# Local attention: mask added by VectorE, probabilities scaled ahead of transposing, values stationary in column halves, and a new order of the mixer

## The chip, the cores and the metric

The kernel runs on one core of a Trainium2 chip. The metric is the device time of one execution in microseconds. Three executions of the kernel before gave 978.89, 980.45 and 980.59 us; the median is 980.45 us. A trace was taken of one further execution.

## What is computed

The reference is a two-layer encoder on 256 positions of width 1024. Each layer is a half-step feed-forward block, a mixer, and a second half-step feed-forward block, each followed by a layer norm:

```python
x = layer_norm(ALPHA * x + 0.5 * swiglu(x, ffn1_w_in[l], ffn1_w_out[l]), ln_g[l, 0], ln_b[l, 0])
mix = hybrid_mixer(x, cos, sin, mask, w_in[l], w_out[l], ...)
x = layer_norm(ALPHA * x + mix, ln_g[l, 1], ln_b[l, 1])
x = layer_norm(ALPHA * x + 0.5 * swiglu(x, ffn2_w_in[l], ffn2_w_out[l]), ln_g[l, 2], ln_b[l, 2])
```

The mixer projects x to two groups of heads and applies rotary positions. The first group is differential attention (4 heads, each with two score maps). The second is local attention: 8 query heads in two groups of 4, one key and value head for each group, a window of 128 positions to either side, and a sink logit for each query head that takes part in the softmax's maximum and sum. The two results stand side by side and go through one output projection:

```python
s = jnp.where(mask[None, :, None, None, :, :], s, -jnp.inf)
m = jnp.maximum(jnp.max(s, axis=-1, keepdims=True), sk)
e = jnp.exp(s - m)
p = e / (jnp.sum(e, axis=-1, keepdims=True) + jnp.exp(sk - m))
o = jnp.einsum('bnhgqk,bnkhd->bnqhgd', p.astype(v.dtype), vb)
```

## The kernel before

The 256 positions are two tiles t of 128 rows. Activations that a matmul takes as its stationary operand lie transposed in `xx`, which holds for each of the 8 chunks k of the width a rounded high part and the remaining low part. Every weight tile of 128x1024 is loaded by a DMA from SyncE's queue (L72), rounded by ScalarE to `wh` (L74), and its rest is taken by VectorE as `wl` (L75); these two run at a lowered priority. A product is then three matmuls: high by high, high by low, low by high. `raw` has 5 buffers, `wh` and `wl` have 9 each, and a weight is asked for 8 tiles ahead.

TensorE's order is the program's own order. The other engines' order is set by the scheduler of the framework, with a few blocks raised in priority.

The mixer's order on TensorE is the table `ORDER` (L47 to L54). Its words are: `P nm t c`, c quarter-projections (L448 to L450) of dq, dk, dv, sq or sk for tile t; `T`, the transposing of a projected and rotated tile (`transp`, L475); `S d` and `S s`, scores of the differential (`sd`) and of the local group (`ss`), 4 heads' maps in a unit u; `A`, transposing of the differential probabilities; `V`, their product with the values (`od`); `W q n`, three steps of the local group's product with the values for tile q; `Y t h`, transposing of half h of the mixer's result y into `xx`; `O t c`, c of the 8 chunks of the output projection (`ao`, L666); `X` and `Z`, transposing of x; `G`, loading of the norm's factors.

The lines the change touches:

- `swa_scores` (L516): a unit is 12 matmuls for 4 maps in two PSUM banks, one bank for each key head v. Key head 0 lies on partitions 0 to 63, key head 1 on 64 to 127, so that the matmuls of the two (L486) use different row halves of the array. After the 3 matmuls of a map, a matmul of `identb` with the bf16 `mask` (L525), on all 128 rows, adds minus 2^100 to the masked block. VectorE takes the maxima (L528), ScalarE the exponentials and their sums (L542), VectorE the reciprocal of the sums (L545, L546).
- `swa_pv` (L582): unscaled exponentials are transposed (L554), copied to `pTs` by ScalarE (L556), and used as the stationary operand; the values `vs` stream past with 64 columns (L598, 16 matmuls in float32 for a tile). VectorE multiplies the result by the reciprocals and writes it to y (L613). `Y t 1` then transposes that half of y (L260), and ScalarE and VectorE write its two parts to `xx` (L262, L263).
- the start: `load_xt` (L156) brings x transposed in four pieces of two chunks, each followed by one weight tile; the positions and the rotary frequencies are loaded by GpSimd's queue (L191, L193).
- the rotary arithmetic of a projection is `rope` (L454 to L473), at the ordinary priority.

## Time and profile before

| | |
|---|---|
| median of three runs | 980.45 us (978.89 to 980.59) |
| the profiled execution | 979.31 us, span of its trace 977.5 us |
| TensorE matmul busy | 966.5 us, 99% |
| TensorE weight load busy | 823.5 us, 84% |
| VectorE busy | 664.6 us, 68% |
| ScalarE busy | 510.6 us, 52% |
| GpSimd busy | 18.3 us, 2% |
| bytes moved by DMA | 176.44 MB, 181 GB/s on average |

A matmul's row in the trace lasts longer than the next one has to wait, since matmuls are pipelined. What a matmul costs is therefore read from the distance between the start of one and the start of the next, not from its length; the same holds, to a lesser degree, for VectorE and ScalarE, where rows overlap by some 0.08 us.

### The profile page before, as it was taken

Reading aid. Unit: us, or ns where it says so; the run is one execution under the profiler, and the core shown is the slowest. Engines: PE = TensorE matmul, PEld = TensorE weight load, DVE = VectorE, ACT = ScalarE, POOL = GpSimd, SP = SyncE. Lnnn points to the kernel's source line nnn. Section 1 sums busy time; section 2 is a strip of 40 time slices with the busy share of each in tenths; the row PEclk is TensorE's granted clock in tenths of the full one; section 3 lists DMA queues with packets and bytes.
Section 4 is the critical chain, followed back from the end, with each engine's and each line's share of the span. In section 5 each row is a group of like instructions: output and inputs, shape, how many; then the busy total and the mean of one; then the engine's idle time right before and its main releaser. Section 6 shows DMA issues by size and latency. Waiting matters only on the chain.

```text
span 977.5 us, 13872 instructions
## 1 busy us (share of the span) xinstructions
PE 966.5 (99%) x5199; PEld 823.5 (84%) x5199; DVE 664.6 (68%) x1057; ACT 510.6 (52%) x887; POOL 18.3 (2%) x30
## 2 busy tenths in 40 slices
PE   8999999999999999999999999999999999999997
PEld 5888888888888888888888888888888888888886
DVE  6887654598838766664587667548896587766534
ACT  4767553346744655553356555433576456555420
POOL 1000000000000000000000000000000000000000
PEclk9999999999999999999999999999999999999999
DMA  7986555375305755555377555554742167555521
GB/s 267 317 291 195 193 176 192 128 237 194 109 25 162 269 191 185 186 190 194 113 243 248 187 184 191 187 193 128 250 137 76 44 230 248 190 193 186 181 65 44
DMA packets 50323, 176.44 MB, mean 181 GB/s; under 512 B 5824, under 2 KB 7376, under 8 KB 50256
## 3 DMA queue, kind: packets, MB, share of 16 engines
q1 hardware_dynamic: 50192, 175.54, 53.4%
q8 instruction: 41, 0.67, 0.3%
q0 software_dynamic: 64, 0.02, 0.1%
q14 instruction: 26, 0.21, 0.1%
HBM read 174.48 MB, written 1.05 MB: 180 GB/s over the span
## 4 chain that ended last, share of the span: by engine, by line
PE 98%; DMA 1%; DVE 1%; SPq 0%; ACT 0%; issue 0%; DVEq 0%
PE acc L383 24%; PE hg L333 14%; PE hu L333 14%; PE hb L301 9%; PE hu L335 7%; PE hg L335 7%; PE ao L666 5%; PE ss L486 2%; PE os L598 1%; DMA raw<-in_f_b_dram 1%; PE pj_sq L448 1%; PE pj_sq L450 1%; PE pj_dq L450 1%; PE pj_dq L448 1%; PE pj_sq L449 1%; PE pj_dv L448 1%
## 5 line engine op out<-in xcount | busy, mean ns | idle before, releaser
L75 DVE TENSOR_TENSOR wl<-raw,wh 128x1024 fp32r<-128x1024 f32 (+1 forms) x317 | 385.3, 1219 | 209.4 <-ACT wh L74 205.3
L74 ACT CAST wh<-raw 128x1024 fp32r<-128x1024 f32 (+1 forms) x317 | 331.8, 1049 | 324.7 <-PE acc L383 123.7
L383 PE MATMUL acc<-wh,g 128*128 128x512 f32 (+1 forms) x748 | 192.7, 377 | 0.0
L383 PEld LDWEIGHTS acc<-wh,g 128*128 128x128 f32 x748 | 136.0, 188 | 25.8
L333 PE MATMUL hg<-xx,wh 128*128 128x512 f32 x576 | 144.8, 393 | 0.0
L333 PE MATMUL hu<-xx,wh 128*128 128x512 f32 x576 | 144.2, 392 | 0.0
L333 PEld LDWEIGHTS hg<-xx,wh 128*128 128x128 f32 x576 | 103.6, 189 | 18.6
L333 PEld LDWEIGHTS hu<-xx,wh 128*128 128x128 f32 x576 | 103.6, 189 | 18.5
L383 PE MATMUL acc<-wl,g 128*128 128x512 f32 (+1 forms) x374 | 111.3, 377 | 0.0
L335 PEld LDWEIGHTS hg<-xx,wl 128*128 128x128 f32 x576 | 78.6, 190 | 5.7
L335 PEld LDWEIGHTS hu<-xx,wl 128*128 128x128 f32 x576 | 78.6, 190 | 5.6
L335 PE MATMUL hu<-xx,wl 128*128 128x256 f32 x576 | 80.3, 282 | 0.0
L335 PE MATMUL hg<-xx,wl 128*128 128x256 f32 x576 | 80.3, 282 | 0.0
L383 PEld LDWEIGHTS acc<-wl,g 128*128 128x128 f32 x374 | 68.9, 188 | 13.2
L301 PE MATMUL hb<-wh,xx 128*128 128x512 f32 x256 | 72.7, 401 | 2.2 <-ACT wh L74 2.2
L301 PEld LDWEIGHTS hb<-wh,xx 128*128 128x128 f32 x256 | 49.0, 193 | 14.3 <-ACT wh L74 4.3
L301 PE MATMUL hb<-wl,xx 128*128 128x512 f32 x128 | 40.4, 398 | 0.3 <-DVE wl L75 0.3
L666 PE MATMUL ao<-wh,xx 128*128 128x512 f32 x128 | 37.7, 398 | 0.0
L342 ACT CAST g<-tl 128x256 fp32r<-128x256 f32 x72 | 28.9, 402 | 6.8 <-DVE tl L340 6.8
L340 DVE TENSOR_TENSOR tl<-tl 128x256 f32<-128x256 f32 x72 | 30.6, 425 | 2.3
L337 DVE TENSOR_TENSOR tl<-hu,tl 128x256 f32<-128x256 f32 x72 | 30.1, 417 | 2.2 <-ACT tl L336 2.2
L343 DVE TENSOR_TENSOR g<-tl,g 128x256 fp32r<-128x256 f32 x72 | 30.1, 419 | 2.0 <-ACT g L342 1.9
(184 smaller groups left out, 980.8 us busy)
## 6 DMA issues: line engine op xcount, KB each, us to landing
raw<-in_f_in_dram SPq DMA_DIRECT2D x144, 512.0 KB, 3.8
raw<-in_f_out_dram SPq DMA_DIRECT2D x88, 512.0 KB, 3.5
raw<-in_m_in_dram SPq DMA_DIRECT2D x36, 512.0 KB, 3.6
raw<-in_f_b_dram SPq DMA_DIRECT2D x31, 512.0 KB, 3.5
raw<-in_m_out_dram SPq DMA_DIRECT2D x16, 512.0 KB, 4.4
lng<-in_ln_g_dram SPq DMA_DIRECT2D x6, 512.0 KB, 5.7
lnb<-in_ln_b_dram SPq DMA_DIRECT2D x6, 512.0 KB, 5.8
xr<-in_x_tr_dram SPq DMA_DIRECT2D x4, 256.0 KB, 8.7
```

What stands on the lines that cost most here:

```text
L74: nc.scalar.copy(wh[:, s], raw[:, s])
L75: nc.vector.tensor_tensor(wl[:, s], raw[:, s], wh[:, s].bitcast(F32), ALU.subtract)
L301: mm(hb[s], xx[:, k, g, t, :], ww[:, 512 * s : 512 * s + 512], start=(k == 0 and e == 0), stop=(k == KT - 1 and e == 2))
L333: mm(hs[s], wh[:, k * P : (k + 1) * P], xx[:, k], start=(k == 0), stop=False)
L335: mm(hs[s][:, 1, :], wl[:, k * P : (k + 1) * P], xx[:, k, 0], start=False, stop=(k == KT - 1))
L337: dv.tensor_tensor(tl[:, s], hs[s][:, 0, :], tl[:, s], ALU.add)
L340: dv.tensor_tensor(gv, tl[:, 0], gv, ALU.mult)
L342: nc.scalar.copy(gs[q][:, jj, 0, :], gv)
L343: dv.tensor_tensor(gs[q][:, jj, 1, :], gv, gs[q][:, jj, 0, :].bitcast(F32), ALU.subtract)
L383: mm(a, g, ww[:, s], start=(k == 0 and e == 0), stop=(k == JT - 1 and e == 2))
L448: mm(o, xx[:, k, 0, t, :], wh[:, s], start=(k == 0), stop=False)
L666: mm(acc[t][h], xx[:, k, g, t, :], ww[:, s], start=(k == 0 and e == 0), stop=(k == KT - 1 and e == 2))
```

## The change

The core of the diff:

```diff
-identb = cp.tile([P, P], BF16, name="identb")
-nc.gpsimd.tensor_copy(identb, ident)
-mask = cp.tile([P, 2, P], BF16, name="mask")
+mask = cp.tile([P, 2, P], F32, name="mask")
...
-                        qk(sc[v][:, i, :], sqT, skT, a, 2 * u + i, 0, qt, False)
-                        mm(sc[v][:, i, ob], identb, mask[:, qt, :], start=False, stop=True)
+                        qk(sc[v][:, i, :], sqT, skT, a, 2 * u + i, 0, qt)
                 mx = sp.tile([P, 4], F32, tag="mx", name=f"mxs{nm}")
                 for v in range(2):
+                    mb = mask[:, qt : qt + 1, :].to_broadcast([P, 2, P])
+                    dv.tensor_tensor(sc[v][:, :, ob], sc[v][:, :, ob], mb, ALU.add)
                     dv.tensor_reduce(mx[:, 2 * v : 2 * v + 2], sc[v], AX.X, ALU.max)
...
                 dv.reciprocal(rc, rc)
-            return e, rc
+                for v in range(2):
+                    for i in range(2):
+                        q = 2 * v + i
+                        dv.tensor_scalar(e[:, v, i, :], e[:, v, i, :], rc[:, q : q + 1], None, ALU.mult)
+            return e
...
-                        mm(o[:, hd, :], pTs[q][:, i, k, :], vs[:, k, v * HD : (v + 1) * HD], start=(k == 0), stop=(k == 1))
+            def mm_(u):
+                for k in range(2):
+                    for v in range(2):
+                        a = slice(v * HD, (v + 1) * HD)
+                        mm(o[a, 2 * u : 2 * u + 2, :], vs[:, k, a], pTs[u, v][:, :, k, :], start=(k == 0), stop=(k == 1))
...
-                        for u, (e, rc) in enumerate(units):
-                            rv = rc.rearrange("p (v i) -> p v i", v=2)[:, :, :, None].to_broadcast([P, 2, 2, HD])
-                            dv.tensor_tensor(yv[:, :, u], ov[:, :, u], rv, ALU.mult)
+                        dh = xx[:, 4:8, 0, qt, :]
+                        nc.scalar.copy(dh, o)
+                        dv.tensor_tensor(xx[:, 4:8, 1, qt, :], o, dh.bitcast(F32), ALU.subtract)
...
+        def rope(*a):
+            with tc.high_priority():
+                return rope_(*a)
...
-    for c in range(4):
-        load_xt(c)
-        W.upto(c + 1)
+    for k0, k1 in ((0, 1), (1, 2), (2, 4), (4, 6), (6, 8)):
+        load_xt(k0, k1)
+        W.upto(k1)
...
     def rotary():
+        nc.sync.dma_start(pos_i, pos)
+        nc.sync.dma_start(inv_t, inv.partition_broadcast(P))
```

In words: the 32 mask matmuls go, and VectorE adds the mask in PSUM, two additions for a unit. VectorE multiplies the exponentials by the reciprocals ahead of their transposing, four multiplications for a unit. In the product with the values, the values are now the stationary operand, 64 columns of them for each key head, so that the two key heads' results come on partitions 0 to 63 and 64 to 127 of one bank, already transposed; the probabilities stream past with 256 columns, 8 matmuls for a tile. ScalarE and VectorE write that straight to `xx`, and `Y t 1` with its transposes is gone. The rows of the output projection's weight that belong to this half are gathered to match, by two DMAs of 64 partitions for a tile. The first two chunks of x come in pieces of their own, the positions and frequencies are loaded later, from SyncE's queue, and the rotary arithmetic is raised in priority. `ORDER` is another table; its last part is now

```python
A 0 1; T sq 0; T sk 0; V 0; S s 0; P sq 1 1; A 1 1; A 1 0; P sq 1 1; S s 0; V 1; Y 0; G; T sq 1; O 0
2; S s 1; W 0 0; O 0 1; Y 1; W 0 1; W 0 2; O 0 1; S s 1; O 1 1; W 1 0; O 0 1; O 1 1; O 0 1; W 1 1; O 0 2; W 1 2;
O 1 4; Z; O 1 2
```

On TensorE, the first local score unit of layer 0 stands so in the program before (`ss0000` and `ss0001` are the banks of the two key heads, `identb` the identity that the mask goes through):

```order
L486 MATMUL ss0000_2510<-skT0_1865,sqT00_1863 128x256 x2
L486 MATMUL ss0000_2510<-skT0_1865,sqT01_1864 128x256
L525 LDWEIGHTS identb_142
L525 MATMUL ss0000_2510<-mask_144,identb_142 128x128
L486 MATMUL ss0001_2511<-skT0_1865,sqT00_1863 128x256 x2
L486 MATMUL ss0001_2511<-skT0_1865,sqT01_1864 128x256
L525 LDWEIGHTS identb_142
L525 MATMUL ss0001_2511<-mask_144,identb_142 128x128
```

and so in the changed program, ahead of a quarter of sq's projection for the second tile:

```order
L497 MATMUL ss0000_2496<-skT0_1867,sqT00_1865 128x256 x2
L497 MATMUL ss0000_2496<-skT0_1867,sqT01_1866 128x256
L497 MATMUL ss0001_2497<-skT0_1867,sqT00_1865 128x256 x2
L497 MATMUL ss0001_2497<-skT0_1867,sqT01_1866 128x256
L455 MATMUL pj_0_sq1_2438<-wh82_1997,xx_78 128x512
```

The matmuls of the two row halves now follow each other with nothing between (the first rows of the block, which come twice in a unit, are shown once).

On VectorE, between the rotation of sq for the second tile (`m1`, `m2`, `r_0_sq1`) and the low part of its transposed form (`sqT01`), the program before has these rows around the second score unit (`mxs001` are its maxima, `wl92` a split of a weight, `y01` the differential group's result for the second tile):

```order
L75 TENSOR_TENSOR wl92_2573<-raw92_2571,wh92_2572 128x1024
L470 TENSOR_TENSOR r_0_sq1_2560<-m1_0_sq1_2558,m2_0_sq1_2559 128x2x4x64
L528 TENSOR_REDUCE mxs001_2628<-ss0010_2610 128x2
L575 TENSOR_SCALAR f01_2585<-sq01_2584 128x4
L528 TENSOR_REDUCE mxs001_2628<-ss0011_2611 128x2
```

and the changed program has these:

```order
L80 TENSOR_TENSOR wl91_2420<-raw91_2418,wh91_2419 128x1024
L470 TENSOR_TENSOR m1_0_sq1_2559<-pj_0_sq1_2438,cos_t_182 128x512
L473 TENSOR_TENSOR m2_0_sq1_2560<-pj_0_sq1_2438,sin_t_183 128x8x32 x2
L539 TENSOR_TENSOR ss0010_2566<-ss0010_2566,mask_170 128x2x128
L477 TENSOR_TENSOR r_0_sq1_2561<-m1_0_sq1_2559,m2_0_sq1_2560 128x2x4x64
L540 TENSOR_REDUCE mxs001_2580<-ss0010_2566 128x2
L539 TENSOR_TENSOR ss0011_2567<-ss0011_2567,mask_170 128x2x128
L557 TENSOR_TENSOR rs000_2526<-ds000_2521,es000_2516 128x4
L80 TENSOR_TENSOR wl92_2652<-raw92_2650,wh92_2651 128x1024
L270 TENSOR_TENSOR xx_78<-tr_y000_2630,xx_78 128x4x128
```

A mask addition has come between the rotation's parts, and the split of weight 92 stands ahead of the low part of the first transposed y (`xx_78<-tr_y000`), which the output projection takes.

Further on in VectorE's list of the changed program, the scaling of the first two units' probabilities (`esw000`, `esw001`) has these places:

```order
L558 RECIPROCAL rs000_2526<-rs000_2526 128x4
L492 TENSOR_TENSOR sqT01_1866<-tq_0_sq1_2641,sqT00_1865 128x4x128
L562 TENSOR_SCALAR esw000_2520<-esw000_2520,rs000_2526 128x256 x4
L557 TENSOR_TENSOR rs001_2596<-ds001_2591,es001_2586 128x4
L539 TENSOR_TENSOR ss0100_2674<-ss0100_2674,mask_170 128x2x128
L539 TENSOR_TENSOR ss0101_2675<-ss0101_2675,mask_170 128x2x128
```

The four multiplications of a unit are new in the list, and the transposes of `W 0 0` and `W 0 1` read what they write.

More of the change, by code (lines that the diff above doesn't have):

```diff
@@ L69, in _make @@
         n = 512 if i == 0 else 1024
+        src = self.srcs[i]
+        rows = src if isinstance(src, tuple) else (src,)
         for c in range(0, 1024, n):
             s = slice(c, c + n)
-            nc.sync.dma_start(raw[:, s], self.srcs[i][:, s])
+            for q, r in enumerate(rows):
+                h = P // len(rows)
+                nc.sync.dma_start(raw[q * h : (q + 1) * h, s], r[:, s])
             with self.tc.high_priority(-LATER):
@@ L134, in encoder_kernel @@
         srcs += [m_in[l, 3, q] for q in range(4)]
-        srcs += [m_out[l, k * P : (k + 1) * P, :] for k in range(KT)]
+        srcs += [m_out[l, k * P : (k + 1) * P, :] for k in range(KT // 2)]
+        srcs += [tuple(m_out[l, 512 + 256 * v + HD * n : 512 + 256 * v + HD * (n + 1), :] for v in range(2))
+                 for n in range(KT // 2)]
         srcs += [f2_b[l, k] for k in range(KT)]
@@ L481, in transp, with qk @@
             dv.tensor_tensor(dst[1][:, :, a], tr[:, 0:n, :], dst[0][:, :, a].bitcast(F32), ALU.subtract)
-        def qk(o, q, k, a, h, kh, qt, last):
+        def qk(o, q, k, a, h, kh, qt):
             b = slice(qt * P, (qt + 1) * P)
             for i, (m, n) in enumerate(((0, 0), (0, 1), (1, 0))):
-                mm(o, q[m][a, h, b], k[n][a, kh, :], start=(i == 0), stop=(last and i == 2))
+                mm(o, q[m][a, h, b], k[n][a, kh, :], start=(i == 0), stop=(i == 2))
         def diff_scores(qt, u):
@@ L654, in do_w @@
             if n == 0:
-                sw[q] = swa_pv(q, units["s", q], y[q])
+                sw[q] = swa_pv(q, units["s", q])
             sw[q](n)
@@ L692, in mixer @@
             elif op == "W":
-                ok = num("S", "s", ar[0]) > min(ar[1], 1) and (ar[1] == 0 or num("W", ar[0], ar[1] - 1))
+                ok = (ar[1] < 2 or all(full(nm, ar[0]) for nm in heads)) and num("S", "s", ar[0]) > min(ar[1], 1) and (ar[1] == 0 or num("W", ar[0], ar[1] - 1))
             elif op == "Y":
-                ok = all(full(nm, ar[0]) for nm in heads) and (num("W", ar[0], 2) if ar[1] else num("V", ar[0]))
+                ok = all(full(nm, ar[0]) for nm in heads) and num("V", ar[0])
             elif op == "O":
-                ok = num("Y", ar[0], 0) and num("G") and (rows(ar[0]) + ar[1] <= 4 or num("Y", ar[0], 1))
+                ok = num("Y", ar[0]) and num("G") and (rows(ar[0]) + ar[1] <= 4 or num("W", ar[0], 2))
             elif op == "Z":
```

50 lines of the change are left out of this document (18 added, 32 removed).

## The prediction

> **What bounds the kernel now.** I read the page first (span, busy shares, the chain that ended last), then TensorE's waits after the start, then TensorE's timeline in the mixer, and at last the rows of VectorE, which gets the new work.
>
> ```profile
> span 977.5 us, 13872 instructions
> PE 966.5 (99%) x5199; PEld 823.5 (84%) x5199; DVE 664.6 (68%) x1057; ACT 510.6 (52%) x887; POOL 18.3 (2%) x30
> PE 98%; DMA 1%; DVE 1%; SPq 0%; ACT 0%; issue 0%; DVEq 0%
> ```
>
> The waits of TensorE between 15 and 977 us have one row:
>
> ```profile
> PE hb L301 <- DVE wl L75: 0.3, 1, 0.3
> ```
>
> So TensorE sets the time: 98% of the chain is its matmuls, and after the first 15 us it waits 0.3 us in all. A matmul taken from its list is worth the distance from its start to the next start, as long as no other engine comes to be late. Every saving must be set against what VectorE then does.
>
> **The change part by part.** These are starts and lengths of TensorE's rows in layer 0:
>
> ```profile
> 230.72 0.39 PE L449 MATMUL pj_dv<-wl,xx 128*128 128x512 f32 x1
> 230.94 0.39 PE L450 MATMUL pj_dv<-wh,xx 128*128 128x512 f32 x1
> ...
> 231.26 0.98 PE L486 MATMUL sd<-dkT,dqT 64*128 64x256 f32 x12
> ...
> 232.17 0.39 PE L448 MATMUL pj_sk<-wh,xx 128*128 128x256 f32 x1
> 232.39 0.28 PE L449 MATMUL pj_sk<-wl,xx 128*128 128x256 f32 x1
> 232.51 0.28 PE L450 MATMUL pj_sk<-wh,xx 128*128 128x256 f32 x1
> ...
> 250.95 1.97 PE L568 MATMUL od<-vd,pTd 128*128 128x128 f32 x16
> 252.67 0.47 PE L448 MATMUL pj_sq<-wh,xx 128*128 128x512 f32 x1
> ...
> 255.10 0.62 PE L486 MATMUL ss<-skT,sqT 64*128 64x256 f32 x3
> 255.65 0.23 PE L525 MATMUL ss<-mask,identb 128*128 128x128 bf16 x1
> ...
> 257.84 0.61 PE L260 MATMUL tr_y<-ident,y 128*128 128x128 f32 x4
> 258.20 0.47 PE L448 MATMUL pj_sq<-wh,xx 128*128 128x512 f32 x1
> ...
> 273.46 3.68 PE L598 MATMUL os<-vs,pTs 128*128 128x64 f32 x32
> 276.98 0.61 PE L260 MATMUL tr_y<-ident,y 128*128 128x128 f32 x4
> ```
>
> *The masks.* A differential unit and a local unit have the same 12 matmuls on alternating row halves; only the masks stand between the local ones. The first takes 232.17 - 231.26 = 0.91 us, or 0.08 a matmul; the second takes 257.84 - 255.10 = 2.74 us. Its first three matmuls take 0.55, or 0.18 each, so the masks cost more than their own 0.16: they keep the two halves from overlapping. Without them a local unit should cost what the differential one does. Leaving the half-array also costs something: the matmul behind `sd` waits 232.39 - 232.17 = 0.22, where 0.12 is usual (232.51 - 232.39); a masked unit ended on the full array and did not pay it. The saving is 2.74 - 0.91 - 0.10 = 1.73 us for each of 8 units: **-13.8**.
>
> The Trainium skill, page "TensorEngine Tiling (Array Packing)", section Key Properties, says that switching the tiling mode drains TensorE, which speaks for removing the masks and against the new column halves. The trace bears it out: the 0.10 above, and 231.26 - 230.94 = 0.32 at the entry against 230.94 - 230.72 = 0.22. Without the rule, 8 x 0.10 here and the 1.2 of the column halves below would fall away, and the sum would be 2.0 lower.
>
> *Transposes of y's second half.* Four blocks of 258.20 - 257.84 = 0.36 us go, one for each tile and layer: **-1.4**. ScalarE's and VectorE's writing to `xx` is the same in kind and number.
>
> *Values stationary in halves.* The old product of a tile has 32 rows (two for each float32 matmul) and takes 276.98 - 273.46 = 3.52 us. The new one has 8 matmuls, so 16 rows, with 256 columns in float32, a form the trace does not have:
>
> ```profile
> L568 PE MATMUL od<-vd,pTd 128*128 128x128 f32 x64 | 7.8, 275 | 0.0
> L449 PE MATMUL pj_sk<-wl,xx 128*128 128x256 f32 x32 | 9.1, 283 | 0.0
> ```
>
> A float32 row of 128 columns lasts about as long as a rounded one of 256, so I take a float32 row of 256 columns to cost what a rounded one of 512 does, 0.22 (the low end is 0.12, that of 256). Without overlap that is 16 x 0.22 = 3.5, no gain. But pairs of rows lie on the two column halves in turn, as triples in `sd` lie on the row halves. If a row starts, in order, as soon as its own half is free, 12 rows in triples fill 9 steps of 0.91 / 9 = 0.10, which fits the 0.12 of a lone row better than 6 steps of 0.15 would; and 8 rows in pairs fill 5 steps. Two groups of 8 then cost 10 x 0.22 = 2.2. The new blocks switch mode at both ends; there are 3 a layer (one tile's two steps stand together), so 6 x 2 x 0.10 = 1.2 in all. With overlap: 4 x (3.52 - 2.2) - 1.2 = 4.1, **-4.1**; without it 1.2 slower; with the low price and overlap 4 x (3.52 - 1.2) - 1.2 = 8.1 faster. I take the overlap at 0.22, by the `sd` row.
>
> *VectorE.* It gets 16 mask additions and 32 multiplications and loses 8 products (L613). Where that matters is the stretch of the mixer's end. Its rows there, and the busy time of TensorE, its weight loads and VectorE in 10 us windows:
>
> ```profile
> 232.65 1.28 DVE L499 TENSOR_REDUCE mxd<-sd 128x2 f32<-128x512 f32 x2
> 248.75 0.75 DVE L466 TENSOR_TENSOR m_sq<-pj_sq,sin_t 128x256 f32<-128x256 f32 x2
> 254.49 0.17 DVE L575 TENSOR_SCALAR f<-sq 128x4 f32<-128x4 f32 x1
> 254.57 0.15 DVE L622 TENSOR_TENSOR nlam<-le 128x1 f32<-128x1 f32 x1
> 255.99 1.13 DVE L580 SCALAR_TENSOR_TENSOR y<-od,f,gsb 128x128 f32<-128x128 f32 x4
> 301.24 3.49 DVE L75 TENSOR_TENSOR wl<-raw,wh 128x1024 fp32r<-128x1024 f32 x3
> ...
> 250.00:260.00 10.00, 10.00 (x68) 8.39 (x67) 8.79 (x22) 6.65 (x19) 1.02 (x1) 1.00 0.38 118
> 260.00:270.00 10.00, 10.00 (x63) 8.11 (x62) 7.25 (x24) 6.92 (x25) 1.01 (x1) 1.00 0.26 98
> 270.00:280.00 10.00, 10.00 (x75) 8.50 (x75) 4.29 (x14) 4.81 (x18) 0.00 (x0) 1.00 0.02 4
> ```
>
> VectorE is 88% and 73% busy in the windows where the first local scores fall, and 43% in the next. I take the stretch from the first local scores to the transposes of `W 0 1`, and count VectorE's list of the changed program there: 6 mask additions at 0.75 / 2 = 0.38 (2.3); 6 maxima at 0.64 (3.8); 8 products for y at 0.28 (2.2); 2 weight splits at 1.16 (2.3); the rotation of sq, two at 0.64 and two at 0.38 (2.0); 2 low parts at 0.64 (1.3); 8 multiplications; 20 small ones at 254.57 - 254.49 = 0.08 (1.6). A multiplication by a column has its bounds here:
>
> ```profile
> L427 DVE TENSOR_SCALAR gsb<-gsb 128x128 f32<-128x128 f32 x2 | 0.4, 222 | 2.1 <-DMA gsb<-in_sub_g_dram 2.1
> L513 DVE SCALAR_TENSOR_TENSOR ed<-ed,wt 128x256 f32<-128x256 f32 x16 | 7.0, 480 | 0.1
> DVE f L578 <- POOL f L576: 3.0, 4, 1.1
> ```
>
> 0.22 with half the columns, 0.48 with the same columns and two inputs; I take 0.30, nearer the first since it is the same operation (8 x 0.30 = 2.4). GpSimd's power makes VectorE wait 3.0 / 4 = 0.75 a time, twice; as other rows stand between, I take half (0.7). The sum is 18.6 us.
>
> TensorE in the same stretch, with a quarter projection or a chunk at 6 x 0.22 = 1.35: two quarters and three chunks 6.75; two score units at 0.91 and two switches 2.2, and the rest of the first 0.4; `V 1` at 252.67 - 250.95 = 1.72 and a switch 1.8; seven transposing blocks (A, A, Y, T, two in `W 0 0`, Y) at about 0.38, 2.7. That is 13.9. VectorE's list is longer by 4.7. The first transposes of `W 0 1` need only half of the last unit's multiplications (0.6), so the wait is 4.1 a layer: **+8.2**. It shows as TensorE waiting for sq's rotation, for the low part of y behind a weight split, for `sqT` and for `esw`. The bounds are +2 (the two splits moved out and the multiplication at 0.22) and +13 (the multiplication at 0.48 and the whole 0.75). Behind this stretch I cost the new work at nothing: the 43% row is its cover.
>
> *Order, rotation's priority, output weights, positions.* The moved projections cost what they did. The priority lets a rotation pass weight splits, which only helps TensorE here. Four more DMA issues a layer go into SyncE's queue; DMA's share was 0.26 and 0.02 in two of the windows above. The positions now stand in SyncE's queue behind x, and VectorE's list waits for them with a PSUM addition and weight splits behind it:
>
> ```profile
> x_in<-in_x_tok_dram SPq DMA_DIRECT2D x2, 512.0 KB, 7.9
> ```
>
> Even 7.9 us there cost nothing: weights are asked for 8 tiles ahead, and a tile keeps TensorE for 8 x 0.22 + 8 x 0.12 = 2.7. Without that lead it would cost up to 7.9.
>
> *The start.* TensorE's second weight tile is what it waits for:
>
> ```profile
> 12.19 1.04 ACT L74 CAST wh<-raw 128x1024 fp32r<-128x1024 f32 x1 [4.31 <-DMA raw<-in_f_b_dram]
> 13.29 1.00 PE L301 MATMUL hb<-wh,xx 128*128 128x512 f32 x2 [0.29 <-ACT wh L74]
> 11.00:12.00 1.00, 1.00 (x4) 0.71 (x3) 0.96 (x2) 0.00 (x0) 0.00 (x0) 1.00 1.08 418
> ```
>
> Two pieces of x of 256 KB stood ahead of it; now two of 128 KB do. 256 KB at 418 GB/s is 0.6 us: **-0.6**. Since the first tile's matmuls ended just before, more than 1.5 is excluded by the same rows; nothing is the other end.
>
> **The sum.** 979.3 (the profiled execution) - 13.8 - 1.4 - 4.1 - 0.6 + 8.2 = 967.6. That execution lies within the three runs (978.9 to 980.6), 1.1 below their median, so 968 is what I give for a median.
>
> **Rivals.**
>
> *VectorE is never late.* If the splits of weights fall into gaps and TensorE's own waits shift to where VectorE has room, the +8.2 goes: 967.6 - 8.2 = 959.4, given as 959. For it speaks the 43% row, against it the list, in which two splits stand between the score units whatever the gaps are.
>
> *The column halves do not overlap.* Then the product costs 3.5 a tile and 1.2 for switches: 967.6 + 4.1 + 1.2 = 972.9, given as 973. For it: no row of this trace has column halves, and both halves write one PSUM bank, where the two halves of `sd` write two.
>
> *The column halves overlap fully.* 8 steps of 0.22 a tile give 1.76 where I have 2.2, 1.8 in all: 967.6 - 1.8 = 965.8, given as 966. The `sd` row, 0.91 rather than 6 x 0.12 = 0.72, speaks against it. The Trainium skill, page "TensorEngine Tiling (Array Packing)", section When to Use Tiling, names this very swap of stationary and streaming with column tiling, with up to a factor of two; no row here shows it.
>
> *VectorE's new work is exposed whole.* In a score unit the scores, two additions, two maxima, exponentials, sums, four multiplications and transposes follow each other. If TensorE stands at each unit for what is new, 2 x 0.38 + 4 x 0.48 = 2.7 us, then 8 units lose 21.6 on top: 967.6 + 21.6 = 989.2, given as 989. It decides from the point at which the distance from a unit's scores to its `W` is less than the chain; the table has 6 us and more between (at `W 1 1`, four chunks and the two transposes of `W 1 0`), so I hold it for unlikely.
>
> **How the numbers follow.** The forecast of 968 has a chance of 0.43, VectorE never late 0.22, no overlap 0.22, full overlap 0.08, exposed whole 0.05. The range takes in 959 and 973, the bounds of VectorE's cost around the forecast (+2 and +13: 961 to 972), and a little above 973 for no overlap with VectorE later than forecast: 959 to 975. A measurement of this kernel can tell about 0.2%, 2 us, from no change. All cases but the last lie 6 us or more below 980.45: faster 0.94, same 0.01, slower 0.05.
>
> **What would show it.** In the profile after: a local unit's 12 matmuls in about 0.9 us; 32 fewer mask rows and 16 fewer transposes; 16 rows of `os` in 2.2 a tile (3.5 if the halves do not overlap); waits of TensorE for VectorE of about 4 us a layer between the first local scores and `W 0 1`, in `tq_sq`, `ao`, `ss` and `tps`; the second weight tile's first matmul near 12.7 us. The prediction is wrong if a unit without masks still takes over 2 us, or if TensorE's waits in the mixer are nothing or over 13 us in all.

## The result, and the profile after

| | before | after |
|---|---|---|
| median | 980.07 us (4 runs, 978.89 to 980.59) | 964.15 us (4 runs, 964.05 to 964.51) |
| the profiled execution | 979.31 us, span 977.5 | 964.06 us, span 962.2 |

The ratio is 0.984, with a 95% interval of 0.9823 to 0.9857: 15.9 us faster. From the page of the changed kernel, the span, the busy times and the chain that ended last:

```profile
span 962.2 us, 13695 instructions
PE 947.0 (98%) x5087; PEld 801.8 (83%) x5087; DVE 673.7 (70%) x1099; ACT 509.4 (53%) x887; POOL 16.9 (2%) x27
PE 91%; DVE 5%; ACT 1%; issue 1%; DMA 0%; POOL 0%; SPq 0%; DVEq 0%; ACTq 0%
```

TensorE still sets the time, but VectorE now has 5% of the chain. Before, TensorE waited 0.3 us after the first 15 us; now its waits between 15 and 960 us are these (total, times, longest):

```profile
PE tq_sq L489 <- DVE wt L522: 1.6, 2, 0.8
PE ss L497 <- DVE sqT L492: 1.6, 2, 0.8
PE ao L678 <- DVE xx L270: 1.0, 2, 0.5
PE ao L678 <- ACT xx L269: 0.7, 2, 0.4
```

Each stands there twice, once a layer. None is for a weight, so the output weights that are gathered by two DMAs cost TensorE no wait here. TensorE's timeline in layer 0 shows the local units and the new product (start, length, and the idle time in front where there is some):

```profile
255.27 0.98 PE L497 MATMUL ss<-skT,sqT 64*128 64x256 f32 x12
256.18 2.05 PE L584 MATMUL od<-vd,pTd 128*128 128x128 f32 x16
...
263.45 0.50 PE L497 MATMUL ss<-skT,sqT 64*128 64x256 f32 x2
264.75 0.98 PE L497 MATMUL ss<-skT,sqT 64*128 64x256 f32 x10 [0.80 <-DVE sqT L492]
265.65 1.09 PE L570 MATMUL tps<-ident,esw 128*128 128x128 f32 x8
...
269.70 1.95 PE L614 MATMUL os<-pTs,vs 128*64 128x256 f32 x16
271.58 0.73 PE L678 MATMUL ao<-wh,xx 128*128 128x512 f32 x2
...
281.76 1.08 PE L614 MATMUL os<-pTs,vs 128*64 128x256 f32 x8
282.78 0.73 PE L678 MATMUL ao<-wh,xx 128*128 128x512 f32 x2
```

A local unit that doesn't wait takes 256.18 - 255.27 = 0.91 us, where it took 2.74. The 16 rows of one tile's product take 271.58 - 269.70 = 1.88, where 32 rows took 3.52; the other tile's, in two blocks of 8, take 1.02 and 1.01. Together that is 3.91 us a layer instead of 7.04. A third unit's scores stand still after their first two rows, for the low part of `sqT`: the unit takes 265.65 - 263.45 = 2.20 us, so 1.3 us are lost, of which the view of waits, which goes by the ends of the rows, shows 0.80.

The mixer of layer 0 in one window each (its length, TensorE's busy time, weight loads, VectorE, ScalarE, GpSimd, clock, DMA), before and after:

```profile
195.47:305.15 109.68, 109.68 (x652) 92.42 (x650) 84.77 (x171) 63.15 (x144) 4.02 (x4) 1.00 0.41 136
```

```profile
192.42:295.98 103.56, 101.07 (x595) 81.85 (x594) 89.52 (x192) 62.71 (x144) 4.01 (x4) 1.00 0.46 145
```

The mixer is 6.1 us shorter, that of layer 1 (109.69 to 103.72) 6.0. It also begins 195.47 - 192.42 = 3.05 us sooner, all of it won in the first 34 us: the second product of the first block starts at 30.25 us instead of 33.27. What lies between is as long as before. So 12.1 + 3.0 of the 15.2 us between the two profiled executions are placed.

### The profile page after: what moved, and what is told of

It is laid out like the page before. It is cut to its first block, busy times and chain, and to the rows that moved or that the text cites. A ratio compares the mean times of both kernels' runs of the same rounds, so it can differ in the third digit from the quotient of the medians.

```text
span 962.2 us, 13695 instructions
## 1 busy us (share of the span) xinstructions
PE 947.0 (98%) x5087; PEld 801.8 (83%) x5087; DVE 673.7 (70%) x1099; ACT 509.4 (53%) x887; POOL 16.9 (2%) x27
## 4 chain that ended last, share of the span: by engine, by line
PE 91%; DVE 5%; ACT 1%; issue 1%; DMA 0%; POOL 0%; SPq 0%; DVEq 0%; ACTq 0%
PE acc L390 25%; PE hg L340 14%; PE hu L340 14%; PE hb L308 9%; PE hu L342 7%; PE hg L342 7%; PE ao L678 4%; DVE wl L80 1%; PE tps L570 1%; PE os L614 1%; PE pj_dq L457 1%; PE pj_dv L457 1%; PE pj_dq L455 1%; PE pj_dv L456 1%; PE pj_dk L457 1%; PE pj_dv L455 1%
## 5 line engine op out<-in xcount | busy, mean ns | idle before, releaser
L678 PEld LDWEIGHTS ao<-wh,xx 128*128 128x128 f32 x128 | 22.6, 188 | 9.6 <-issue 2.3
```

The costliest lines, as they stand in the source:

```text
L678: mm(acc[t][h], xx[:, k, g, t, :], ww[:, s], start=(k == 0 and e == 0), stop=(k == KT - 1 and e == 2))
```

## The experiments

Times are medians; a ratio is to runs of the kernel before that were taken beside it, with its 95% interval. The changed kernel has 964.15 us and 0.984.

### The masks alone

The kernel before, with this edit (and the mask in float32, for VectorE) and nothing else:

```diff
...
-                        qk(sc[v][:, i, :], sqT, skT, a, 2 * u + i, 0, qt, False)
-                        mm(sc[v][:, i, ob], identb, mask[:, qt, :], start=False, stop=True)
+                        qk(sc[v][:, i, :], sqT, skT, a, 2 * u + i, 0, qt, True)
...
+                    dv.tensor_tensor(sc[v][:, :, ob], sc[v][:, :, ob], mb, ALU.add)
...
```

> The kernel before with its old order, in which only the mask is added by VectorE in place of the 32 matmuls. Theory of the prediction: a local unit falls from 2.74 to about 0.91 us, so TensorE loses 13.8 us of work; VectorE gets 16 additions of about 0.38 us and no scaling, so at most 2 to 3 us of that come back as waits: about 966 to 969 us by a run of the kernel before of 979 to 980. Rival A (the masks are worth no more than their own 0.16 us each, and the rows of the two halves do not overlap without them): 32 x 0.16 = 5.1 us, about 974 to 975. Rival B (VectorE's additions stand exposed between scores and maxima at each unit): over 6 us of waits for VectorE, 972 or more.

Measured: 981.16 us, ratio 1.0016 (1.0004 to 1.0029). It is no faster. The figure of rival B holds (972 or more, with over 6 us of waits), but not its mechanism: TensorE doesn't stand at each unit, but once a layer, at the transposes of sq. TensorE's timeline where the time went, and windows of the same stretch (columns as above; the clock is the third number from the end):

```profile
263.08 0.97 PE L484 MATMUL ss<-skT,sqT 64*128 64x256 f32 x12
268.99 1.08 PE L476 MATMUL tq_sq<-ident,r_sq 128*128 128x128 f32 x4 [4.93 <-DVE r_sq L468]
269.72 1.20 PE L665 MATMUL ao<-wh,xx 128*128 128x512 f32 x2
...
275.20 0.61 PE L665 MATMUL ao<-wh,xx 128*128 128x512 f32 x2
```

```profile
263.00:269.00 6.00, 1.07 (x15) 0.81 (x13) 5.55 (x19) 2.86 (x15) 1.01 (x1) 0.89 0.24 87
269.00:275.00 6.00, 6.00 (x22) 5.17 (x23) 1.46 (x6) 4.36 (x15) 0.00 (x0) 0.54 0.05 15
```

A unit does take 0.9 us. But in the old order the transposes of sq stand right behind the second unit, and the rotation that they read is far back in VectorE's list: 268.99 - 263.08 - 0.91 = 5.0 us are lost. Then the clock is granted at 0.54, and until 274.7 two rows of the output projection take 0.85 to 1.0 us instead of 0.45, which loses 2.6 more. 5.0 + 2.6 eat the 6.9 that a layer saves, and a little more. The mask matmuls had been the cover under which VectorE rotated sq. The Trainium skill, page "TensorE: Matmul & The Clock Gate", section "What's actually happening", halves the clock after an idle window of about 3.4 us; this wait of 5.0 agrees. Shorter stops bring the drop as well, as the kernels with a new table show below.

### The start, in two halves

The kernel before with x in five pieces, and the kernel before with the two small loads moved to SyncE's queue:

```diff
-    for c in range(4):
-        load_xt(c)
-        W.upto(c + 1)
+    for k0, k1 in ((0, 1), (1, 2), (2, 4), (4, 6), (6, 8)):
+        load_xt(k0, k1)
+        W.upto(k1)
```

> The kernel before with only its start's loads of x changed: five pieces instead of four. Theory of the prediction (fewer bytes stand ahead of the second weight tile): 0.6 us faster by the forecast, or as much as the 3.0 us by which the whole change reached the mixer of layer 0 sooner, if the pieces alone do it; then the second weight's rounding comes near 9 us and the wait of 1.58 us at 7.94 us is gone. Rival (the small loads of positions and frequencies on GpSimd's queue hold up the first transfers): less than 0.5 us here, and the gain in the next kernel.

```diff
-    nc.gpsimd.dma_start(pos_i, pos)
...
-    nc.gpsimd.dma_start(inv_t, inv.partition_broadcast(P))
...
     def rotary():
+        nc.sync.dma_start(pos_i, pos)
+        nc.sync.dma_start(inv_t, inv.partition_broadcast(P))
```

> The kernel before with only the positions and frequencies loaded later, from SyncE's queue. Theory of the prediction: no change at the start, 979 to 980 us, and no wait for them later. Rival (the small loads on GpSimd's queue hold up the first transfers of weights): 1.5 to 3 us faster, with the first weight's second half arriving about 2 us sooner.

Measured: the pieces 979.05 us, 0.9999 (0.9990 to 1.0007); the moved loads 976.99 us, 0.9977 (0.9968 to 0.9986), so 1.4 to 3.1 us faster: both are what the rival said, that the small loads on GpSimd's queue hold up the first transfers. Two rows of the kernel before, and the same two of the one with the loads moved: SyncE's fourth load of x, and ScalarE's rounding of the first weight tile's halves (start, length).

```profile
5.02 2.49 SPq L159 DMA_DIRECT2D xr<-in_x_tr_dram  x1
...
7.27 0.62 ACT L74 CAST wh<-raw 128x512 fp32r<-128x512 f32 x1 [1.76 <-DMA raw<-in_f_b_dram]
```

```profile
4.89 1.25 ACT L74 CAST wh<-raw 128x512 fp32r<-128x512 f32 x2 [2.67 <-DMA raw<-in_f_b_dram]
5.01 0.55 SPq L159 DMA_DIRECT2D xr<-in_x_tr_dram  x1
```

With GpSimd's two loads of 1 and 16 KB under way, SyncE took 2.49 us to issue a load that otherwise takes 0.55, and the second half of the first weight could be rounded at 7.27; without them both halves are rounded back to back from 4.89. The weights behind come sooner as well: the rounding of the second tile starts at 9.66 us instead of 12.19. The second product then starts at 31.02 us instead of 33.27. With the pieces alone the second weight tile also comes sooner (10.16), but TensorE then waits 2.46 us for the low part of the first, which stands in VectorE's list behind the second piece of x, and the second product starts at 32.72. So the start's gain is the moved loads. Why SyncE's issue and the transfers are slow beside GpSimd's isn't shown by these rows.

### The column halves

First the changed kernel with the loops of the new product swapped, then the same with both key heads on one column half, which leaves one key group's result out:

```diff
-                for k in range(2):
-                    for v in range(2):
+                for v in range(2):
+                    for k in range(2):
```

> The changed kernel with the two loops of the new product swapped, so that four rows on one column half stand together and then four on the other, instead of pairs in turn; the work is the same. Theory of the prediction (a row starts, in order, as soon as its own half is free): 8 rows in blocks of four fill 7 steps of about 0.21 instead of 5, and the 16 rows of the tile whose two groups stand together 13 instead of 9, so 0.42 + 0.42 + 0.84 us a layer, 3.4 us slower than the changed kernel in all if no other wait covers it. Rival A (the halves overlap by some other rule that does not depend on the order in pairs): no change, within 0.5 us. Rival B (rows never overlap and a row costs 0.12 to 0.13): no change either, and the blocks keep their 1.01 us.

```diff
-                        mm(o[a, 2 * u : 2 * u + 2, :], vs[:, k, a], pTs[u, v][:, :, k, :], start=(k == 0), stop=(k == 1))
+                        mm(o[0:HD, 2 * u : 2 * u + 2, :], vs[:, k, a], pTs[u, v][:, :, k, :], start=(k == 0), stop=(k == 1))
...
-                        nc.scalar.copy(dh, o)
...
+                        nc.scalar.copy(dh, o[0:HD])
...
```

> The changed kernel in which both key heads' rows of the new product go to the same 64 columns of the array, four rows of one and then four of the other; the second head's values overwrite the first's, and partitions 64 to 127 of this half of y are left unwritten, so one key group's result is left out. The number of rows and their shapes stay. Theory A (a row of 256 float32 columns costs about 0.21 us and the two column halves run beside each other, whatever the order): with one half only, the 8 rows of a block cost about 1.8 us instead of 1.02 and the 16 rows 3.4 instead of 1.88, 3.1 us a layer, 6 us in all: about 970. Theory B (such a row costs 0.12 us and rows never overlap): the blocks keep 1.0 and 1.9 us, and the time stays within 0.7 us of the changed kernel's.

Measured: 964.55 us (0.9849, 0.9835 to 0.9862) with the loops swapped, no change; 970.80 us (0.9913, 0.9898 to 0.9928) on one half. The 16 rows of layer 0 with the loops swapped, and on one half:

```profile
269.01 2.00 PE L614 MATMUL os<-pTs,vs 128*64 128x256 f32 x16
270.94 0.73 PE L678 MATMUL ao<-wh,xx 128*128 128x512 f32 x2
```

```profile
271.38 3.67 PE L614 MATMUL os<-pTs,vs 128*64 128x256 f32 x16
274.97 0.73 PE L678 MATMUL ao<-wh,xx 128*128 128x512 f32 x2
```

On one half they take 3.59 us, 0.22 a row; on two halves 1.93 or 1.88, in whichever order the rows come. So the price of a row was right, the halves overlap fully, and the step model of the prediction (each row waits, in order, for its own half) is wrong: by it four rows in a block would have cost 3.4 us more. The starts of the single rows say the same: in the changed kernel the 16 rows start as eight pairs, the two of a pair 0.01 us apart and the pairs 0.22 (the first and second 0.27).

### What the order and the rotation's priority are worth

Four kernels. First, the kernel before with the masks by VectorE and the rotation raised in priority (`rope` under `tc.high_priority()`, as in the change):

> The kernel before with the mask added by VectorE, as in the first experiment, and the rotary arithmetic raised in priority; old order of the mixer, old product. Theory (the mask matmuls were the cover under which the rotation of sq for the second tile was done in time; the only thing that took the gain back was that this rotation stood behind other work in VectorE's list): the wait of 5 us a layer at its transposes falls under 1.5 us, TensorE's clock stays at 1.00 there, and the time is 966 to 970 us. Rival (in the old order the rotation's input itself comes too late, or VectorE has too much to do in that stretch whatever comes first, so that the new order is needed): TensorE still waits 3 us or more a layer, at this or another place, and the time is 973 us or more.

Then the changed kernel with the old table, less `Y t 1`:

```diff
...
-P sq 1 2; A 0 1; T sq 0; T sk 0; V 0; S s 0; P sq 1 1; A 1 1; A 1 0; P sq 1 1; S s 0; V 1; Y 0; G; T sq 1; O 0
-2; S s 1; W 0 0; O 0 1; Y 1; W 0 1; W 0 2; O 0 1; S s 1; O 1 1; W 1 0; O 0 1; O 1 1; O 0 1; W 1 1; O 0 2; W 1 2;
-O 1 4; Z; O 1 2
...
+1; P sq 1 2; A 0 1; T sk 1; T sq 0; T sk 0; V 0; P sq 1 1; A 1 1; A 1 0; S s 0; Y 0; P sq 1 1; G; O 0 1; V 1; S s 0;
+T sq 1; O 0 1; W 0 0; O 0 1; S s 1; W 0 1; W 0 2; Y 1; S s 1; W 1 0; O 0 1; O 1 1; O 0 2; W 1 1; W 1 2; O 0 2; O 1
+6; Z; O 1 1
```

> The changed kernel with the mixer's table of the kernel before (less the transposes of y's second half, which are gone). Theory of the prediction (the order moves work without a cost of its own, and the rotation's priority is what keeps VectorE in time): 964 to 968 us. Rival (the new order is a condition of the gain): TensorE waits 5 us or more a layer for VectorE around the transposes of sq and the second score unit, its clock falls there, and the time is 972 us or more.

Measured: 985.00 us (1.0046, 1.0033 to 1.0060) and 986.10 us (1.0070, 1.0054 to 1.0086). The rival held both times. The priority, which should have brought out the masks' gain, costs some 3 us against the masks alone (1.0046 against 1.0016). TensorE's waits with masks and priority, then with all but the order, and of the latter the timeline at the longest one:

```profile
PE tps L557 <- ACT esw L545: 10.4, 8, 2.9
```

```profile
PE tps L570 <- DVE esw L562: 13.3, 4, 6.5
PE tps L570 <- DVE mxs L547: 7.4, 2, 3.7
```

```profile
260.95 0.62 PE L678 MATMUL ao<-wh,xx 128*128 128x512 f32 x2
268.07 1.54 PE L570 MATMUL tps<-ident,esw 128*128 128x128 f32 x6 [6.49 <-DVE esw L562]
```

The priority brings the rotation in time, and what it pushes back, the first units' maxima and all that hangs on them, is now late: the wait moves from `tq_sq` to `tps`. With the whole change but the old table, the first unit's scores stand at 251.75 us, and its transposes could begin at 261.4, when the two rows at 260.95 are done; VectorE is ready for them at 268.07. Not all of this wait is VectorE's work: in layer 1, where the same wait is 6.45 us, VectorE itself stands idle for 2.44 us of it, for ScalarE, which works through the eight exponentials of both units one behind the other (747.78 to 751.44). In the changed kernel the same scores stand at 250.20 and the transposes at 265.65, 15.4 us behind, and these transposes don't wait. The clock falls here too: it was granted at 0.66 from 265 to 275 us and at 0.88 from 275 to 285 (with masks and priority at 0.66 from 270 to 280). The total is near the prediction's last rival (new work exposed whole, 989 us), and its condition is met, a distance shorter than the chain. But it is not its price of 2.7 us at each of four units: there are two long stops a layer, of 6.5 and 3.7 us, and the lower clock.

The other two are the kernel before with the new table alone, where I put the transposes of y's second half, which it still has, right behind `W t 2`; and that with the masks by VectorE as well:

```diff
...
+A 0 1; T sq 0; T sk 0; V 0; S s 0; P sq 1 1; A 1 1; A 1 0; P sq 1 1; S s 0; V 1; Y 0 0; G; T sq 1; O 0 2; S s 1; W 0
+0; O 0 1; Y 1 0; W 0 1; W 0 2; Y 0 1; O 0 1; S s 1; O 1 1; W 1 0; O 0 1; O 1 1; O 0 1; W 1 1; O 0 2; W 1 2; Y 1 1; O
+1 4; Z; O 1 2
```

> The kernel before with only the new table of the mixer (the transposes of y's second half, which this kernel still has, stand behind the last step of the local product). The masks stay on TensorE. Theory formed from the runs so far (the order moves work without a gain or loss of its own; it pays only by giving VectorE and ScalarE longer between a unit's scores and what reads them): TensorE has nothing to wait for here, so no change: 978 to 981 us. Rival (the new order is better by itself): 975 us or less. Rival (it lengthens some chain of the old program): over 982 us.

> The kernel before with the mask added by VectorE, as in the first experiment, and the new table of the mixer; rotation at its old priority, old product, no scaling. Theory (the masks are worth 13.8 us of TensorE's time, and the new order is the condition for getting it): 979.4 - 13.8 and up to 3 us a layer of waits that are left for VectorE: 966 to 972 us, with TensorE's clock at 1.00 throughout the mixer. Rival (without the rotation's priority the transposes of sq still wait 5 us a layer): 976 us or more.

Measured: 990.80 us (1.0121, 1.0104 to 1.0138) and 981.85 us (1.0030, 1.0017 to 1.0042). My theory fell for both; the rivals (a longer chain in the old program, and sq's transposes that still wait) had them. The new table alone is the slowest kernel of all, in part by the place that I gave `Y t 1`: TensorE stands there until VectorE has written y. Its layer 0 has five gaps of 0.7 to 1.1 us and loses 1.2 to rows at half the rate, together 5.3 of the 6.3 us by which its mixer is longer; the last 1.0 I have not placed. In layer 1, where the clock does not drop, the mixer is 4.7 us longer. With the masks the two largest waits are these (then the longest one in each layer, and the window behind the second):

```profile
PE tq_sq L476 <- DVE r_sq L468: 7.4, 4, 3.2
PE tr_y L258 <- DVE y L612: 2.9, 4, 0.9
...
266.09 0.66 PE L476 MATMUL tq_sq<-ident,r_sq 128*128 128x128 f32 x4 [3.14 <-DVE r_sq L468]
...
746.14 1.11 PE L476 MATMUL tq_sq<-ident,r_sq 128*128 128x128 f32 x4 [3.16 <-DVE r_sq L468]
...
745.00:750.00 5.00, 3.86 (x13) 3.31 (x14) 3.84 (x14) 2.62 (x10) 1.46 (x1) 0.66 0.02 3
```

So in this order, without the priority, the rotation is late again, and in layer 1 a stop of 3.16 us also brings the clock down, which one of 3.14 in layer 0 does not (1.00 from 260 to 280 us). The three edits together:

> The kernel before with the three edits that were tried in pairs so far: the mask added by VectorE, the new table of the mixer, and the rotation's priority; old product, no scaling ahead of transposing, old start. Theory (it takes the order and the priority together to give VectorE's list the time it needs; without the priority the rotation of sq was 3.7 us late in a layer): the wait at the transposes of sq falls under 1 us, what is left are waits of about 1 us each for y behind the old product, and the time is 968 to 974 us, 5 to 11 us better than the kernel before. Rival A (the new product's way of writing its result straight to the transposed form, with no scaling and transposing of y behind it, is a condition too): the two late halves of y cost 1.5 to 2 us each, and the time is 976 us or more. Rival B (VectorE has simply too much to do): waits of 4 us or more a layer in front of sq and the scores, 976 us or more as well.

Measured: 978.14 us, 0.9984 (0.9973 to 0.9994): rival A's figure, though the late halves of y are smaller than it had them; the theory's 968 to 974 is missed. So masks, table and priority together bring 1.8 of the masks' 13.8 us. The waits and the mixer's window:

```profile
PE tr_y L258 <- DVE y L616: 2.9, 4, 0.9
PE tq_sq L480 <- DVE wt L513: 1.6, 2, 0.8
PE ao L669 <- DVE xx L261: 1.0, 2, 0.5
...
195.18:304.04 108.86, 104.84 (x635) 88.10 (x634) 88.65 (x181) 62.57 (x144) 4.02 (x4) 1.00 0.42 142
```

The clock stays at 1.00 and the rotation is in time. What is left are nearly the waits of the changed kernel, and on top the two late halves of y, which by distances between starts cost 0.68 and 1.08 us a layer. From here to the changed kernel the traces differ by 977.17 - 964.06 = 13.1 us: 5.3 and 5.0 in the mixers and 2.8 at the start (33.02 to 30.25). The account of the mixers nearly closes: 6.3 us for the new product, 1.4 for the transposes of y and 2 x 1.76 = 3.5 for the waits in front of them are 11.2, where 10.3 are measured; 0.7 of the 0.9 too much are the rows behind the new product's blocks (below). By this account the scaling of the probabilities, 32 rows on VectorE, costs 0.2 us or nothing; it was not tried by itself.

### What is left of TensorE's waits

VectorE's and ScalarE's rows of the changed kernel ahead of the wait at 264.75:

```profile
260.19 0.61 ACT L491 CAST sqT<-tq_sq 128x512 fp32r<-128x512 f32 x1
...
262.55 0.23 DVE L594 TENSOR_TENSOR f<-f,rd 128x2 f32<-128x2 f32 x2 [0.53 <-POOL f L592]
...
263.69 0.34 DVE L596 SCALAR_TENSOR_TENSOR y<-od,f,gsb 128x128 f32<-128x128 f32 x1
...
264.04 0.66 DVE L492 TENSOR_TENSOR sqT<-tq_sq,sqT 128x512 fp32r<-128x512 f32 x1
```

The high part is ready at 260.8, and the low part could follow; in VectorE's list it stands behind the power that GpSimd takes, the products for y and a split of a weight at 259.53 (1.22 us). Two kernels that compute the same. In the first, the mixer asks for weights 4 tiles ahead, and the splits of four tiles are held back:

```diff
...
+        if i % 158 in (89, 90, 91, 92):
+            nc.gpsimd.tensor_copy(wl[:, 0:1], self.hold)
...
                 transp(r[nm, t], dst[nm][1], dst[nm][0], t, nm)
+                W.hold = sqT[1][:, 0, SEQ - 1 : SEQ]
```

> The changed kernel with the same result, but with the loading and splitting of weights held back at the mixer's end: weights are asked for 4 tiles ahead there instead of 8, and the splits of four weights of a layer can't start ahead of the low part of sqT for the second tile, since a copy of one column by GpSimd into their tile comes first and reads it. Theory of the prediction (VectorE is late because splits of weights stand ahead of the rows that TensorE waits for): of the 4.7 us a layer by which TensorE is held up, 3 to 4 go, and the time is 956 to 959 us. Rival A (VectorE's own chain sets the wait, and the splits fill gaps): no change, within 1.5 us of the changed kernel. Rival B (the weights held back come late for the output projection or the next block): new waits there, 966 us or more.

In the second, only the table is another:

```diff
...
-P sq 1 2; A 0 1; T sq 0; T sk 0; V 0; S s 0; P sq 1 1; A 1 1; A 1 0; P sq 1 1; S s 0; V 1; Y 0; G; T sq 1; O 0
-2; S s 1; W 0 0; O 0 1; Y 1; W 0 1; W 0 2; O 0 1; S s 1; O 1 1; W 1 0; O 0 1; O 1 1; O 0 1; W 1 1; O 0 2; W 1 2;
-O 1 4; Z; O 1 2
+A 0 1; T sk 0; T sq 0; V 0; S s 0; A 1 1; A 1 0; P sq 1 1; S s 0; P sq 1 1; V 1; Y 0; G; T sq 1; O 0 3; W 0 0; Y 1;
+S s 1; W 0 1; W 0 2; O 0 1; S s 1; O 1 1; O 0 1; W 1 0; O 0 2; O 1 1; O 0 1; W 1 1; W 1 2; O 1 4; Z; O 1 2
```

> The changed kernel, the same result, with another table of the mixer's end: the second unit of the first tile's local scores stands a quarter projection earlier, and the first unit of the second tile's stands behind the transposes of the first tile's probabilities and of y instead of ahead of them; the low parts that the scores read have so 1.5 to 2 us more. Theory (what is left of TensorE's waits in the changed kernel, 4.7 us a layer, is a matter of the distance from a step to what reads it): 2 to 3 us a layer go, 957 to 960 us, and the wait of 0.8 us for the low part of sqT is gone. Rival (VectorE's total work in the stretch sets the end, so that the waits only move): 962.5 to 965.5 us, no change.

Measured: late splits 965.33 us (0.9855, 0.9840 to 0.9870), no gain, where the theory had 956 to 959; the other table 959.22 us (0.9791, 0.9778 to 0.9803), as its theory had it, 4.9 us below the changed kernel, whose interval it does not touch, and the fastest of all. The waits of both kernels, with two of VectorE's rows of the first:

```profile
PE tps L573 <- DVE mxs L550: 2.5, 2, 1.3
PE ss L500 <- DVE sqT L495: 2.3, 2, 1.2
PE tq_sq L492 <- DVE wt L525: 1.6, 2, 0.8
PE ao L681 <- ACT xx L272: 1.1, 2, 0.6
...
263.03 0.60 DVE L565 TENSOR_SCALAR esw<-esw,rs 128x256 f32<-128x256 f32 x2
...
270.52 2.35 DVE L83 TENSOR_TENSOR wl<-raw,wh 128x1024 fp32r<-128x1024 f32 x2
```

```profile
PE tq_sq L488 <- DVE r_sq L476: 1.0, 2, 0.5
PE ao L677 <- DVE xx L269: 0.3, 2, 0.2
...
192.17:293.45 101.28, 100.27 (x596) 82.21 (x594) 89.90 (x193) 63.02 (x144) 4.12 (x4) 1.00 0.47 149
```

With four splits, 4.6 us, held back, the low part of `sqT` still comes late: it stands behind the same power and products, and behind the first unit's multiplications (`esw`, the last two at 263.03), which have moved ahead of it. From the first tile's `tq_sq` to the transposes of `W 0 1` TensorE needs 0.8 us less than in the changed kernel (248.06 to 268.01, against 247.75 to 268.48). But the splits now stand further on, two of them at 270.52, ahead of the second tile's maxima, and the transposes of `W 1 0` wait 1.28 us for these. So less work for VectorE in the stretch was worth 0.8 us of the 4.7, and it was lost again where the work went.

With the other table VectorE has the same work in the mixer (89.90 us, 89.52 before), the scores come later behind the transposes that feed them (265.07 - 258.49 = 6.6 us for the second tile, where it was 263.45 - 258.66 = 4.8), and 2.3 us a layer go. Some of VectorE's rows, the third unit's additions and maxima, now fall behind the stretch, so that amount and order were not varied apart here either.

## Why the prediction was right, and where it was not

The forecast was 968 us, in a range of 959 to 975; measured was 964.15. By its own sum, against the profiled executions:

| term | forecast | measured |
|---|---|---|
| masks | -13.8 | -13.8 (a unit at 0.91, as taken) |
| transposes of y's second half | -1.4 | -1.4 (16 rows fewer) |
| values in column halves | -4.1 | -6.3 (2 x (7.04 - 3.91)) |
| start | -0.6 | -3.0 (33.27 to 30.25) |
| VectorE late | +8.2 | +9.4 (2 x 4.7) |
| sum, from 979.3 | 967.6 | 964.2 (profiled: 964.06) |

The 4.7 are the places in layer 0 where a row starts later than its predecessor's usual distance, added up; the mixer's length gives nearly the same, 103.56 - (109.68 - 6.9 - 0.7 - 3.1) = 4.6. The 6.3 leave out that the second row behind each column-half block starts 0.34 us after the first, where 0.23 is usual; with six such blocks, 0.7 us, the product gave 5.6, and by the mixer's length the late part is less by as much. The errors have opposite signs: by the table the product and the start gave 4.6 us more than forecast, the late VectorE cost 1.2 more. That the sum is off by only 3.4 is in part luck.

**The masks** came out as worked, but only as a share of a sum. Alone they bring nothing (981.16), and with the new table and the rotation's priority 1.8 us (978.14). That the masks were also the cover for VectorE's rotation stood nowhere in the prediction, although its profile of before had the sign: TensorE without waits and VectorE 88% busy in the same window.

**The column halves.** The price of a row was right (0.22). The step that failed is the overlap: "if a row starts, in order, as soon as its own half is free". The swapped loops and the single half show that order is of no account, and that the rival with full overlap, which I gave 0.08, is what happens; it was priced at 1.8 us below the forecast and is worth 2.2 (1.5 with the rows behind the blocks). I had read triples in nine steps into the 0.91 us of 12 rows. The trace of before has the single starts, and they say otherwise: the 12 rows of `sd` start as six pairs, at 231.26, 231.48, 231.60, 231.72, 231.84 and 231.95 us, the two of a pair 0.01 apart, and the next row at 232.17. So the halves overlap fully there too, 0.12 a pair, and what makes the unit longer than 6 x 0.12 are 0.10 us behind the first pair and 0.10 behind the last, at the two changes between half and full array. The Trainium skill, page "TensorEngine Tiling (Array Packing)", section When to Use Tiling, names column tiling by two for this swap; here it is 3.59 / 1.88 = 1.9.

**The start.** The step that failed is "256 KB at 418 GB/s is 0.6 us", with more than 1.5 excluded. I had put the moved loads under later waits only, and not asked what they did where they stood. The pieces of x give nothing that can be told; the loads give 2.3 us. What is left of the 3.0 is 0.7, and this point differs by more between traces with the same loads: with the new ones the second product starts between 29.50 and 31.89 us, with the old ones between 33.02 and 34.58. TensorE's second weight tile came first near 11.2 us (the third of four rows from 10.74), not at 12.7.

**VectorE late.** The size was near, in part by luck: of the 4.7 us a layer about 3.4 lie in the stretch that the prediction took, from the first local scores to the transposes of `W 0 1` (250.20 to 268.48), where it had 4.1. Another 1.0 lies ahead of it, at the first tile's `tq_sq` (247.75), which it didn't count. The list of VectorE's rows, 18.0 us to that point, fits (the stretch is 18.3 us long, VectorE busy for 17.5), but the step that failed is to let this list alone set the end: with 15.1 us of VectorE's work in the stretch it is still 17.5 us long (late splits), with 15.4 and another table 16.5. The order of the steps counts as well: the distance in TensorE's list from a step to what reads it, against the way through the other engines. Of the places named, `ao` and `ss` were right; `tq_sq` waits at the first tile and not the second (0.16 late), and `tps` does not wait.

**The order**, costed at "what they did", is the largest lever in this combination: 22 us (986.10 to 964.15) hang on the table, part of them the lower clock; by itself the same table costs 11.8 (990.80). That the rival of 989 would not occur I had put down to 6 us and more between scores and `W`, read at `W 1 1`. There the changed kernel has 280.68 - 273.17 = 7.5 us and no wait; for the first unit it has 15.4, and the 9.7 of the old table are too few.

## What to carry to other kernels

When work is taken from the engine that sets the time, ask which work of the others was hidden under it: here 13.8 us less on TensorE were worth nothing alone and 1.8 us with the table and the priority made anew, and the mixer's edits one, two or three at a time gave between 1.8 us of gain and 11.8 of loss. Price a chain through other engines by the distance between the two rows of the bounding engine, and not only by how busy the other engine is. Look at small loads at the start: what they cost stands in another queue, here in the time that SyncE's loads take to issue and to land.

## What the runs showed of the hardware

- After TensorE had stood still for 5.0 us its clock was granted at 0.54 for the next 6 us and rows came at half the rate, 2.6 us lost. In the kernel with masks and new table a stop of 3.14 us in layer 0 left it at 1.00, and one of 3.16 us in layer 1 was followed by 0.66 from 745 to 750 us. In the kernel with the new table alone the clock fell to 0.83 in the window from 270 to 280 us with no marked wait over 0.9 us, so the length of one wait isn't all that counts.
- 16 float32 rows of 256 columns cost 3.59 us on one column half, and 1.88 or 1.93 on two, in the two orders of the rows that were tried.
- 12 float32 rows on alternating row halves start as six pairs, 0.12 us a pair; a change between half and full array costs 0.10 us in the row at the change and about 0.10 more in the row behind it.
- With two loads of 1 and 16 KB on GpSimd's queue, one issue on SyncE's took 2.49 us instead of 0.55, and the second weight tile could be rounded at 12.19 us instead of 9.66.
